# Out-projection in seven-product units, chained to the feed-forward of a hybrid decoder block

## The chip, the core and the metric

The kernel runs on one core of a Trainium2 chip. Its time is the device time in microseconds (us) of one execution, taken as the median of several runs. The engines have these names: PE is TensorE (matmul), PEld its weight load, DVE is VectorE, ACT is ScalarE, POOL is GpSimd, and SP is SyncE, which here only issues DMAs. [...]

## What is computed

One decoder layer over 2048 tokens with 1024 channels, all in float32:

```
h    = layer_norm(x, ln_in_g, ln_in_b)
proj = h @ w_in + b_in                      # split into q, k, v, su, sv
attn = sliding_window_attention(rope(q), rope(k), v, sinks)      # 512 wide
sgu  = spatial_gating(su, sv, ...)                               # 512 wide
mix  = concat([attn, sgu]) @ w_out + b_out                       # 1024 x 1024
h    = layer_norm(ALPHA * h + mix, ln_mix_g, ln_mix_b)
ffn  = (silu(h @ w_gate) * (h @ w_up)) @ w_down                  # 2816 wide
out  = layer_norm(ALPHA * h + ffn, ln_ffn_g, ln_ffn_b)
```

Each float32 operand of a matmul is split into a high part (rounded to the fp32r format, written by ACT) and a low part (the rest, written by DVE); a product is then three matmuls: high by high, high by low, low by high.

## The kernel before

The tokens are worked on in 16 tiles of 128 (`NT = 16`). The stages follow each other in time:

1. **Attention stage** (about 0 to 320 us). For each tile: load x, first layer norm (moments on DVE, scale and shift on ACT, affine part on POOL), eight transposes on PE (`x_transpose`), split, in-projection of q, k, v, attention. The split transposed h goes to DRAM (`hTd`), the attention's output too (`mixd[i][0]`).
2. **Gating stage** (`sgu_*`, to about 511 us). Eight groups of two tiles load `hTd` again and do the gating half; its output goes to `mixd[i][1]`. Beside it `load_wo` loads w_out and splits it.
3. **Out-projection** (line 791, `outproj`). One tile after another: `load_mix` brings the tile's mix back and splits it, 48 matmuls of 512 columns (8 blocks of 128 channels, 3 parts, 2 halves of the output) go into `pw` at line 798. Beside it `prep` loads x once more and computes ALPHA times the first layer norm, plus b_out, again (ACT line 139, DVE line 787, POOL line 788). Then line 800 adds `pw`, `normalize` takes the second layer norm (DVE lines 124 to 132, POOL's power at line 127), `affine` multiplies and adds on POOL (lines 142, 143), the result goes to `h2d`, and `h2_transpose` turns it with eight transposes into `h2T`, one tile later.
4. **Feed-forward.** A list of units, each one seven-product (Strassen-Winograd) multiply of 2 x 2 blocks. A gate/up unit `("g", h, f)` gives 128 channels of gate and of up for 1024 tokens; there are 44. A down unit `("d", g, j)` gives two token tiles over one group of hidden channels; there are 24. `unit` (line 924) runs the chain of line 823:

```python
CHAIN = (("a11", "X", True), ("s1", "Z", True), ("s2", "X", False), ("s4", "Z", False),
         ("s3", "X", False), ("a12", "Y", True), ("a22", "X", False))
```

Each product is 4 blocks by 3 parts, so 12 matmuls of 512 columns and 84 in a unit (63 where a group has three blocks). X, Z and Y are PSUM banks; "False" means that the product is accumulated onto what is in the bank, so the bank has to be read by the unit's hook before that product starts. After each product p of a unit, `after(p)` makes the left operand p of the next unit (`Left.make`: 7 splits and 4 sums or differences in a unit, each 128 x 512) and, where the right matrix changes, the right operand for p (`Right.make`: 28 splits and 12 differences in all, 128 x 512 each, into one `bc` buffer for each of seven operands).

The Tile framework simulates the schedule and writes a fixed order for each engine; a buffer is taken over as soon as the tiles that it overlaps are released. Between stages 3 and 4 the pools of the old stage are closed and those of the feed-forward (`psf`, eight PSUM banks; `bc`, `st`, `ot`) are opened. SP's DMA queue and POOL's DMA queue work in the order of issue.

Of the kernel before, what the change touches and what calls it, by code (L numbers as in the profile page):

```python
# [68 lines left out]
def hybrid_block(ctx, tc, x, pos, ln_in_g, ln_in_b, wqkv, wsu, wsv, b_qkv, b_su, b_sv, sinks,  # L69
                 sgu_g, sgu_b, wsT, bs, w_out, b_out, mix_g, mix_b, w_gate, w_up, w_down,  # L70
# [9 lines left out]
    hTd = [dram.tile([P, 2, KT, P], F32, name=f"hTd_{i}") for i in range(NT)]  # L80
    h2d = [dram.tile([P, D], F32, name=f"h2d_{i}") for i in range(NT)]
# [22 lines left out]
    sucol = base.tile([P, NH], F32, name="sucol")  # L104
    xrs = base.tile([P, NT], F32, name="xrs")
# [140 lines left out]
    SP.dma_start(bcol, sgu_b)  # L246

# [445 lines left out]
    wp = pool(front, "wp", 6)  # L693
# [17 lines left out]
    wo = {}  # L711

    def load_wo(k):
        r = raw(f"rwo{k}")
        SP.dma_start(r, w_out[k * P:(k + 1) * P, :])
        if k < 6:
            t = wp.tile([P, 2, D], F32R, tag="w", name=f"wo{k}")
            split_w(t[:, 0, :], t[:, 1, :], r, A, V)
            wo[k] = [t[:, :, :512], t[:, :, 512:]]
        else:  # L720
            wo[k] = []
            for c in range(2):
                t = ap_.tile([P, 2, 512], F32R, tag="a", name=f"wo{k}_{c}")
                split_w(t[:, 0, :], t[:, 1, :], r[:, c * 512:(c + 1) * 512], A, V)
                wo[k].append(t)

    mixs = {}

    def load_mix(i):
        r = raw(f"rm{i}")  # L730
        for j in range(2):
            SP.dma_start(r[:, j * 512:(j + 1) * 512], mixd[i][j].rearrange("p k t -> p (k t)"))
        m = [ap_.tile([P, 2, 512], F32R, tag="a", name=f"m{i}_{a}") for a in range(2)]
        for a in range(2):
            split_w(m[a][:, 0, :], m[a][:, 1, :], r[:, a * 512:(a + 1) * 512], A, V)
        mixs[i] = m

    for gi in range(NG):
# [10 lines left out]
        if gi + 1 == NG:  # L749
            load_wo(6)  # L750
            load_wo(7)
            load_mix(0)
# [9 lines left out]
        if 1 <= gi < 7:  # L762
            load_wo(gi - 1)
    a2.close()
    a2w.close()


    accp = pool(front, "accp", 4)
    trp = pool(front, "trp", 2)
    rp = pool(ctx, "rp", 4, side="right")  # L770
    wr = pool(ctx, "wr", 8, side="right")

    ag, ab = g_in, b_in
# [3 lines left out]
    V.scalar_tensor_tensor(ab, ab, ALPHA, rb, ALU.mult, ALU.add)
    mg = bcast(mix_g, "mg")
    mb = bcast(mix_b, "mb", ap_, "a")

    acc = {}

    def prep(i):
        ac = accp.tile([P, D], F32, tag="acc", name=f"acc{i}")
        SP.dma_start(ac, x[i * P:(i + 1) * P, :])
        x_normalize(ac, i)
        V.tensor_tensor(ac, ac, ag, ALU.mult)
        PL.tensor_tensor(ac, ac, ab, ALU.add)
        acc[i] = ac

    def outproj(i):
        m = mixs.pop(i)
# [78 lines left out]
    class Right:  # L871
# [52 lines left out]
    def unit(name, nk, left, right, hooks, after=None):  # L924
        bank = {}
        for n, (p, x_, first) in enumerate(CHAIN):
# [9 lines left out]
            if after:  # L936
                after(p)
# [229 lines left out]
```

## Time and profile before

| what | value |
|---|---|
| median of 3 runs | 2055.69 us (2055.38 to 2062.29) |
| profiled execution, its own time | 2054.37 us |
| span of the profiled execution | 2052.7 us |
| PE busy | 1956.4 us, 95% of the span |
| DVE busy | 1431.7 us, 70% |
| ACT busy | 754.0 us, 37% |
| POOL busy | 442.6 us, 22% |
| mean TensorE clock granted | 0.982 |

The span lies within the profiled execution's own time; 1.67 us are outside it. Matmuls are pipelined, so the mean of one (390 ns and more) is longer than the step from one to the next; the step is read from runs of many matmuls.

### The profile page before, as it was taken

How to read it: one execution, taken by the hardware profiler on the slowest of the kernel's cores; microseconds unless marked ns; L12 is line 12 of the kernel's file. 1: busy time of each engine (PE TensorE's matmuls, PEld its weight loads, DVE VectorE, ACT ScalarE, POOL GpSimd, SP SyncE). 2: the span in 40 equal slices, each digit the busy share in tenths (PEclk: the TensorE clock that was granted, in tenths of full speed). 3: DMA queues.
4: the chain of work that ended last, by engine and by line, in shares of the span. 5: the costliest groups of instructions: out<-in, count | busy, mean ns of one | idle time of the engine just before them, and what ended most of it. 6: DMA issues, size and time to landing. Idle time of an engine off the chain costs nothing.

```text
span 2052.7 us, 24699 instructions
## 1 busy us (share of the span) xinstructions
PE 1956.4 (95%) x9230; PEld 1611.6 (79%) x9230; DVE 1431.7 (70%) x2353; ACT 754.0 (37%) x1468; POOL 442.6 (22%) x378
## 2 busy tenths in 40 slices
PE   6898899999999779999999999999999999999997
PEld 4777778999778668888888888888888886887875
DVE  8888884745766875555555865555556869769997
ACT  4556663211322353333333533333334324224220
POOL 4576743110667510000000000000000000000212
PEclk9999999999999989999999999999999999999998
DMA  6224259855556342122122331221212656545432
GB/s 228 78 108 149 77 153 196 185 103 133 181 189 203 101 158 82 72 92 83 72 93 69 126 124 72 93 83 72 92 64 92 239 202 232 180 172 184 165 113 103
DMA packets 137008, 267.57 MB, mean 130 GB/s; under 512 B 8244, under 2 KB 79924, under 8 KB 133304
## 3 DMA queue, kind: packets, MB, share of 16 engines
q1 hardware_dynamic: 90024, 196.79, 28.2%
q0 software_dynamic: 46864, 69.21, 12.2%
q8 instruction: 72, 1.18, 0.3%
q14 instruction: 48, 0.39, 0.1%
HBM read 175.79 MB, written 90.18 MB: 130 GB/s over the span
## 4 chain that ended last, share of the span: by engine, by line
PE 65%; DVE 11%; issue 7%; DMA 4%; ACT 2%; POOL 2%; SPq 0%; POOLq 0%; DVEq 0%; ACTq 0%
PE X_g L932 21%; PE Z_g L932 11%; PE X_d L932 8%; PE Y_g L932 5%; PE Z_d L932 4%; PE pu L564 4%; PE pw L798 3%; PE psv L526 3%; PE Y_d L932 2%; DMA acc<-in_x 1%; DMA h2d<-acc 1%; ACT pb L404 1%; DVE da L1022 1%; DVE b_d L897 1%; PE pm L577 1%
## 5 line engine op out<-in xcount | busy, mean ns | idle before, releaser
L833 ACT ACTIVATE ws<-s 128x512 fp32r<-128x512 f32 x176 | 109.9, 627 | 314.6 <-PE Z_g L932 156.7
L982 POOL DMA_DIRECT2D aD<-x x44 | 23.6, 536 | 857.2 <-DVE x L980 837.8
L798 PE MATMUL pw<-wo,m 128*128 128x512 f32 x768 | 180.0, 394 | 0.0
L798 PEld LDWEIGHTS pw<-wo,m 128*128 128x128 f32 x768 | 144.1, 189 | 29.6
L834 DVE TENSOR_TENSOR ws<-s,ws 128x512 fp32r<-128x512 f32 x176 | 121.0, 690 | 54.1 <-ACT ws L833 52.9
L932 PE MATMUL Z_g<-t1t_h,ws 128*128 128x512 f32 x528 | 137.4, 396 | 0.3 <-DVE ws L834 0.3
L932 PE MATMUL Y_g<-b21t_h,wa 128*128 128x512 f32 x528 | 137.2, 394 | 0.0
L932 PE MATMUL X_g<-t2t_h,ws 128*128 128x512 f32 x528 | 130.8, 395 | 3.7 <-ACT x L962 3.7
L932 PE MATMUL Z_g<-b22t_h,ws 128*128 128x512 f32 x528 | 131.6, 398 | 1.7 <-ACT ws L833 1.7
L932 PE MATMUL X_g<-b11t_h,wa 128*128 128x512 f32 x528 | 131.7, 397 | 0.0
L932 PE MATMUL X_g<-t3t_h,ws 128*128 128x512 f32 x528 | 130.3, 395 | 0.2 <-ACT x L962 0.2
L932 PE MATMUL X_g<-t4t_h,wa 128*128 128x512 f32 x528 | 130.0, 395 | 0.0
L833 ACT ACTIVATE ws_d<-s_d 128x512 fp32r<-128x512 f32 (+1 forms) x96 | 55.7, 593 | 186.5 <-PE X_d L932 51.0
L932 PEld LDWEIGHTS Z_g<-b22t_h,ws 128*128 128x128 f32 x528 | 100.6, 191 | 25.8 <-ACT ws L833 2.2
L932 PEld LDWEIGHTS X_g<-t2t_h,ws 128*128 128x128 f32 x528 | 99.4, 188 | 27.2 <-ACT x L962 4.2
L834 DVE TENSOR_TENSOR wa<-rw,wa 128x512 fp32r<-128x512 f32 x132 | 90.2, 685 | 42.0 <-ACT wa L833 41.9
L932 PEld LDWEIGHTS Z_g<-t1t_h,ws 128*128 128x128 f32 x528 | 100.3, 190 | 24.5 <-DVE ws L834 1.0
L932 PEld LDWEIGHTS X_g<-b11t_h,wa 128*128 128x128 f32 x528 | 99.9, 189 | 23.2
L932 PEld LDWEIGHTS X_g<-t3t_h,ws 128*128 128x128 f32 x528 | 99.4, 188 | 23.8 <-ACT x L962 0.7
L932 PEld LDWEIGHTS Y_g<-b21t_h,wa 128*128 128x128 f32 x528 | 99.3, 188 | 23.5 <-ACT wa L833 0.2
L932 PEld LDWEIGHTS X_g<-t4t_h,wa 128*128 128x128 f32 x528 | 99.5, 188 | 23.1
L980 DVE TENSOR_TENSOR x<-X_g,x 128x512 f32<-128x512 f32 x44 | 30.4, 691 | 119.8 <-PE X_g L932 119.8
(224 smaller groups left out, 4111.0 us busy)
## 6 DMA issues: line engine op xcount, KB each, us to landing
rw<-in_w_gate SPq DMA_DIRECT2D x44, 512.0 KB, 3.8
rw<-in_w_up SPq DMA_DIRECT2D x44, 512.0 KB, 4.8
aD<-x POOLq DMA_DIRECT2D x44, 512.0 KB, 2.9
hTd<-hT SPq DMA_DIRECT2D x16, 1024.0 KB, 3.9
hTg<-hTd POOLq DMA_DIRECT2D x16, 1024.0 KB, 10.2
accd<-da POOLq DMA_DIRECT2D x32, 512.0 KB, 2.9
ra<-aD SPq DMA_DIRECT2D x16, 1024.0 KB, 7.2
da<-accd SPq DMA_DIRECT2D x32, 512.0 KB, 3.3
```

Of the source, the lines that this page charges most:

```text
L404: A.activation(pb, pb, AF.Exp, bias=nm[:, h:h + 1], scale=SCALE, accum_out=sm[:, h:h + 1])
L526: PE.matmul(pv_, t[:, a, k, :], wsv_t[k][:, b, :], start=(k == 0 and n == 0), stop=(k == KT - 1 and n == 2))
L564: PE.matmul(pu[:, j, :], wsu_t[k][:, a, hs], t[:, b, k, :], start=(k == 0 and n == 0), stop=(k == KT - 1 and n == 2))
L577: PE.matmul(pm[:, h].rearrange("p b t -> p (b t)"), z[:, a, hs], wsp[:, h].rearrange("p b t -> p (b t)"), start=(a == 0), stop=(a == 1))
L798: PE.matmul(po[:, c * 512:(c + 1) * 512], m[k // 4][:, a, kc], wo[k][c][:, b, :], start=(k == 0 and n == 0), stop=(k == KT - 1 and n == 2))
L833: A.activation(hi, src, AF.Copy)
L834: V.tensor_tensor(lo, src, f32b(hi), ALU.subtract)
L897: V.tensor_tensor(dst[:, k], a[:, k], b[:, k], ALU.subtract)
L932: PE.matmul(bank[x_], lt[:, a, k, :], rt[:, b, k, :], start=(first and k == 0 and m == 0), stop=(k == nk - 1 and m == 2), skip_group_check ...
L980: V.tensor_tensor(v["x1"], ps, v["x1"], ALU.mult)
L982: PL.dma_start(aD[g][h][:, e, :], v["o"].rearrange("p a t -> p (a t)"))
L1022: V.tensor_tensor(s, ps, s, ALU.add)
```

## The change

The out-projection becomes eight more units of the list, `("o", 0, j)`, ahead of the gate/up units: each is one seven-product multiply of two token tiles (left, from `mixd`) by w_out's four quarters (right). Three of the seven right operands (`b11`, `t1`, `t2`) are made in the gating stage by `wo_early`, in groups 2 and 4; the other four (`b22`, `t3`, `b21`, `t4`) are made when the gating stage has ended.

h, the output of the first layer norm, is stored to DRAM from the attention stage (`hd`, one DMA for each tile, in `x_transpose`), and loaded as the unit's accumulator with b_out/ALPHA added on POOL; `prep` goes. The second norm's scale and shift go to ACT (`o_hooks`, a new small DVE instruction makes the shift) and its result z, without the affine part, is stored as `zd`. `z_transpose` turns z in the next unit, after its products s4 and a12, and ACT applies the affine part by channel while it reads the transposes (`mcol`, 128 columns at a time). The affine part by rows, which the down units' accumulators need, is done later by `z_affine`: in gate/up units 3 to 18 of the first half, one tile in each unit is loaded, multiplied and added on POOL, and stored to `h2d` by POOL's queue.

The pools of the front stages move to the right side of SBUF, `wr` has 7 buffers instead of 8, and the last norm's rows are loaded later into the buffers of the second norm's. The diff, cut to its core:

```diff
+    hd = [dram.tile([P, D], F32, name=f"hd_{i}") for i in range(NT)]
+    zd = [dram.tile([P, D], F32, name=f"zd_{i}") for i in range(NT)]
...
-    bsvp = pool(front, "bsvp", 1)
+    pst = ExitStack()
+    ap_ = pool(front, "ap", 8, side="right")
+    rawp = pool(front, "rawp", 4, side="right")
+    cst = pool(front, "cst", 3, side="right")
+    bsvp = pool(front, "bsvp", 1, side="right")
     bsv = bsvp.tile([P, SGW], F32, name="bsv")
-    pst = ExitStack()
-    rawp = pool(front, "rawp", 4)
-    cst = pool(front, "cst", 3)
-    ap_ = pool(front, "ap", 8)
...
     def x_transpose(i):
         t = wk.tile([P, 2, KT, P], F32R, tag="hT", name=f"hT{i}")
+        SP.dma_start(hd[i], xt[i])
...
-    wp = pool(front, "wp", 6)
+    bc = {q: pool(ctx, "bc_" + q, 1) for q in ("b11", "t1", "t2")}
...
+    def wo_quarter(q, k0, n):
+        kk, c = {"b11": (0, 0), "b12": (0, 1), "b21": (1, 0), "b22": (1, 1)}[q]
+        r0 = (4 * kk + k0) * P
+        return w_out[r0:r0 + n * P, c * 512:(c + 1) * 512].rearrange("(k p) c -> p k c", p=P)
+
+    wo_t = {}
+
+    def wo_early(k0):
+        r = {}
+        for q in ("b11", "b12", "b22"):
+            r[q] = raw(f"rwo{q}{k0}").rearrange("p (k c) -> p k c", k=2)
+            SP.dma_start(r[q], wo_quarter(q, k0, 2))
+        for nm in ("b11", "t1", "t2"):
+            if nm != "b11":
+                V.tensor_tensor(r["b11"], r["b12" if nm == "t1" else "b22"], r["b11"],
+                                ALU.subtract)
+            if k0 == 0:
+                wo_t[nm] = bc[nm].tile([P, 2, 4, 512], F32R, tag="b", name=f"{nm}t_o")
+            t = wo_t[nm][:, :, k0:k0 + 2]
+            split_w(t[:, 0], t[:, 1], r["b11"], A, V)
...
-        if gi + 1 == NG:
-            load_wo(6)
-            load_wo(7)
-            load_mix(0)
...
-        if 1 <= gi < 7:
-            load_wo(gi - 1)
+        if gi in (2, 4):
+            wo_early(gi - 2)
...
+    pst.close()
+    front.close()
...
+    wr = pool(ctx, "wr", 7, side="right")
+    psf = pool(ctx, "psf", 8, space=PSUM)
+    st = pool(ctx, "st", 3)
+    ot = pool(ctx, "ot", 4)
+    bc.update({q: pool(ctx, "bc_" + q, 1) for q in ("b22", "t3", "b21", "t4")})
+    oo = ExitStack()
+    bop = pool(oo, "bop", 1)
+    trp = pool(oo, "trp", 2)
...
+            if q in self.t:
+                return
...
+                if "t2" not in r:
+                    r["t2"] = r["b11"]
+                    for k in range(self.nk):
+                        V.tensor_tensor(r["t2"][:, k], src[:, k], r["t2"][:, k], ALU.add)
...
+    bo = bop.tile([P, D], F32, name="bo")
+    SP.dma_start(bo, b_out.partition_broadcast(P))
+    A.activation(bo, bo, AF.Copy, scale=1.0 / ALPHA)
+
+    def load_m(j):
+        t = raw8(f"rm{j}").rearrange("p (e a c) -> p e a c", e=2, a=2)
+        for e in range(2):
+            for a in range(2):
+                SP.dma_start(t[:, e, a], mixd[2 * j + e][a].rearrange("p k t -> p (k t)"))
+        v = t.rearrange("p e a (k t) -> p e a k t", k=4)
+        return Left(f"o{j}", (v[:, 0, 0], v[:, 0, 1], v[:, 1, 0], v[:, 1, 1]), 4)
+
+    def o_right():
+        r = Right("o", lambda q, t: SP.dma_start(t, wo_quarter(q, 0, 4)), 4)
+        r.t.update(wo_t)
+        return r
+
+    hacc, zs = {}, {}
+
+    def load_h(j):
+        hacc[j] = []
+        for e in range(2):
+            t = ot.tile([P, D], F32, tag="o", name=f"hb{j}_{e}")
+            SP.dma_start(t, hd[2 * j + e])
+            PL.tensor_tensor(t, t, bo, ALU.add)
+            hacc[j].append(t)
+
+    def add_block(ac, seen, first, e, c, ps):
+        s = ac[e][:, c * 512:(c + 1) * 512]
+        if first and (e, c) not in seen:
+            V.scalar_tensor_tensor(s, s, ALPHA, ps, ALU.mult, ALU.add)
+        else:
+            V.tensor_tensor(s, ps, s, ALU.add)
+        seen.add((e, c))
+
+    def block_hooks(ac, first, done):
+        seen = set()
+
+        def add(e, c, ps):
+            add_block(ac, seen, first, e, c, ps)
+
+        def y(ps):
+            add(0, 0, ps)
+            done(0)
+
+        def x4(ps):
+            add(1, 0, ps)
+            done(1)
+
+        return {"a11": lambda ps: add(0, 0, ps), "s1": lambda ps: add(1, 1, ps),
+                "s2": lambda ps: add(0, 1, ps), "s4": lambda ps: add(0, 1, ps),
+                "s3": lambda ps: add(1, 1, ps), "a12": y, "a22": x4}
+
+    def o_hooks(j):
+        ac = hacc.pop(j)
+
+        def done(e):
+            i = 2 * j + e
+            mu, rs = moments(ac[e])
+            nmr = small.tile([P, 1], F32, tag="nmr", name=f"nmr{i}")
+            V.tensor_scalar(nmr, mu, rs, -1.0, ALU.mult, ALU.mult)
+            A.activation(ac[e], ac[e], AF.Identity, bias=nmr, scale=rs)
+            SP.dma_start(zd[i], ac[e])
+            zs[i] = ac[e]
+
+        return block_hooks(ac, True, done)
+
+    def z_transpose(i):
+        z = zs.pop(i)
+        for j in range(2):
+            ps = psf.tile([P, 512], F32, tag="f", name=f"ph{i}_{j}")
+            tr = trp.tile([P, 4, P], F32, tag="tr", name=f"tr{i}_{j}")
+            for k in range(4):
+                kk = 4 * j + k
+                PE.transpose(ps[:, k * P:(k + 1) * P], z[:, kk * P:(kk + 1) * P], ident)
+            for k in range(4):
+                kk = 4 * j + k
+                A.activation(tr[:, k], ps[:, k * P:(k + 1) * P], AF.Identity,
+                             bias=mcol[:, 1, kk:kk + 1], scale=mcol[:, 0, kk:kk + 1])
+            SP.dma_start(h2T[i // 4][:, 4 * j:4 * j + 4, (i % 4) * P:(i % 4 + 1) * P], tr)
+
+
+    def z_affine(i):
+        t = ot.tile([P, D], F32, tag="o", name=f"za{i}")
+        SP.dma_start(t, zd[i])
+        affine(t, t, fg[0], fg[1])
+        PL.dma_start(h2d[i], t)
...
+    units = [("o", 0, j) for j in range(NT // 2)]
+    units += [("g", h, f) for h in range(2) for f in range(NF)]
...
+    def load_out(u):
+        if u[0] == "o":
+            load_h(u[2])
+        elif u[0] == "d":
+            load_acc(*u[1:])
...
     ORDER = [p for p, _, _ in CHAIN]
-    prep(0)
-    lefts, rights = {}, {}
-    for i in range(NT):
-        if i + 1 < NT:
-            prep(i + 1)
-        outproj(i)
-        if i + 1 < NT:
-            load_mix(i + 1)
-        if i:
-            h2_transpose(i - 1)
-        if i == NT - 4:
-            lefts[0] = load_left(units[0])
-            rights[0] = load_right(units[0])
+    lefts, rights, fg = {}, {}, []
+
+    lefts[0] = load_left(units[0])
+    rights[0] = load_right(units[0])
+    load_out(units[0])
+    for n_, p in enumerate(ORDER):
+        lefts[0].make(p)
+        if n_ == 1:
             rights[0].fetch()
-    h2_transpose(NT - 1)
-    front.close()
-    pst.close()
-
-    psf = pool(ctx, "psf", 8, space=PSUM)
-    bc = {q: pool(ctx, "bc_" + q, 1) for q in BOF.values()}
-    st = pool(ctx, "st", 3)
-    ot = pool(ctx, "ot", 4)
-    fb_ = pool(ctx, "fb_", 1)
-
     for p in ORDER:
-        lefts[0].make(p)
         rights[0].make(p)
     lefts[1] = load_left(units[1])
-    fg = bcast(ffn_g, "fg", fb_, "fg")
-    fb = bcast(ffn_b, "fb", fb_, "fb")
     for n, u in enumerate(units):
-        new = n + 1 < len(units) and units[n + 1][:2] != u[:2]
+        last = n + 1 == len(units)
+        new = not last and units[n + 1][:2] != u[:2]
         if new:
             rights[n + 1] = load_right(units[n + 1])
             rights[n + 1].fetch()
-        elif n + 1 < len(units):
+        elif not last:
             rights[n + 1] = rights[n]
 
         def after(p):
-            if n + 1 < len(units):
+            if not last:
                 lefts[n + 1].make(p)
             if new:
                 rights[n + 1].make(p)
-
-        if u[0] == "g":
-            hooks, nk = gu_hooks(*u[1:]), 4
-        else:
-            if n and units[n - 1][0] == "g":
-                load_acc(*u[1:])
-            if n + 1 < len(units):
-                load_acc(*units[n + 1][1:])
-            hooks, nk = d_hooks(*u[1:]), GROUPS[u[1]][1] // 2
+            if 0 < n <= NT // 2 and p in ("s4", "a12"):
+                z_transpose(2 * (n - 1) + (p == "a12"))
+
+        if u == ("g", 0, 1):
+            oo.close()
+            fb_ = pool(ctx, "fb_", 2)
+            fg = [bcast(mix_g, "mg", fb_, "f"), bcast(mix_b, "mb", fb_, "f")]
+        if u == ("d", 1, 0):
+            fg = [bcast(ffn_g, "fg", fb_, "f"), bcast(ffn_b, "fb", fb_, "f")]
+        if u[0] == "g" and u[1] == 0 and 3 <= u[2] < 3 + NT:
+            z_affine(u[2] - 3)
+        if not last:
+            load_out(units[n + 1])
+        hooks = {"o": lambda _, j: o_hooks(j), "g": gu_hooks, "d": d_hooks}[u[0]](*u[1:])
+        nk = GROUPS[u[1]][1] // 2 if u[0] == "d" else 4
         unit("_".join(str(x_) for x_ in u), nk, lefts.pop(n), rights.pop(n), hooks, after)
```

## Rows read from the trace of the kernel before

**Rows 1.** The page: busy time of each engine; granted clock over 40 slices.

```profile
span 2052.7 us, 24699 instructions
...
PE 1956.4 (95%) x9230; PEld 1611.6 (79%) x9230; DVE 1431.7 (70%) x2353; ACT 754.0 (37%) x1468; POOL 442.6 (22%) x378
...
PEclk9999999999999989999999999999999999999998
```

**Rows 2.** Windows by stage: length, busy time (instructions) by engine, clock, DMA share, GB/s.

```profile
346.00:500.00 154.00, 153.68 (x1006) 140.52 (x1004) 95.15 (x237) 28.38 (x50) 22.62 (x23) 1.00 0.75 151
...
511.20:759.70 248.50, 220.87 (x996) 180.18 (x995) 187.13 (x224) 82.74 (x127) 135.80 (x64) 0.95 0.50 169
...
780.00:1140.00 360.00, 360.00 (x1551) 291.92 (x1550) 195.31 (x295) 127.35 (x221) 10.13 (x19) 1.00 0.22 81
...
1900.00:2020.00 120.00, 119.59 (x515) 96.56 (x515) 114.41 (x188) 27.32 (x46) 26.44 (x23) 1.00 0.39 135
```

**Rows 3.** Windows with line 798 (out-projection) alone: PE, PEld, then clock, DMA.

```profile
511.20:759.70 248.50, 178.66 (x764) 143.16 (x762) 0.95 0.50 169
700.00:759.70 59.70, 6.04 (x27) 4.68 (x25) 0.80 0.41 138
```

**Rows 4.** The same with line 932 (units) alone.

```profile
700.00:759.70 59.70, 28.49 (x104) 21.73 (x105) 0.80 0.41 138
```

**Rows 5.** The chain that ended last, pieces in order of time: start, length, what.

```profile
639.15 10.92 PE pw L798 x48
...
761.25 2.79 PE X_g L932 x12
```

**Rows 6.** Timeline, end of gating, one tile's transposes, turn to feed-forward: start, length, engine.

```profile
510.16 0.99 PE L577 MATMUL pm<-wsp,z 128*128 128x256 f32 x7
...
513.38 0.69 DVE L588 TENSOR_TENSOR sg<-sg,u 128x512 f32<-128x512 f32 x1
...
638.11 1.04 PE L811 MATMUL ph<-ident,acc 128*128 128x128 f32 x8
...
638.91 1.40 PE L798 MATMUL pw<-wo,m 128*128 128x512 f32 x5
...
711.16 1.97 PE L811 MATMUL ph<-ident,acc 128*128 128x128 f32 x8 [5.12 <-POOL acc L143]
...
723.80 1.97 PE L811 MATMUL ph<-ident,acc 128*128 128x128 f32 x8 [10.67 <-POOL acc L143]
...
725.42 3.71 PE L932 MATMUL X_g<-b11t_h,wa 128*128 128x512 f32 x12
```

**Rows 7.** Groups by line: count, busy us, mean ns, idle before.

```profile
L834 DVE TENSOR_TENSOR ws<-s,ws 128x512 fp32r<-128x512 f32 x176 | 121.0, 690 | 54.1 <-ACT ws L833 52.9
...
L143 POOL TENSOR_TENSOR acc<-acc,mb 128x1024 f32<-128x1024 f32 x16 | 43.2, 2702 | 1.2
L142 POOL TENSOR_TENSOR acc<-acc,mg 128x1024 f32<-128x1024 f32 x16 | 42.4, 2647 | 14.9 <-DVE acc L132 14.9
...
L132 DVE TENSOR_SCALAR acc<-acc,mv,rs 128x1024 f32<-128x1024 f32 x16 | 15.0, 940 | 12.9 <-POOL rs L127 12.9
...
L125 DVE BATCH_NORM_AGGREGATE mv<-st 128x2 f32<-128x12 f32 (+1 forms) x64 | 12.5, 196 | 1.2
```

**Rows 8.** Single lines: shortest, median, longest in ns.

```profile
L166 DVE TENSOR_TENSOR m<-rm,m x32: 679/1448/2892, 495.8 to 689.5; 128x512 fp32r<-128x512 f32 x32
...
L124 DVE BATCH_NORM_STATS2 st<-acc x32: 668/678/689, 533.2 to 716.3; 128x6 f32<-128x512 f32 x32
```

**Rows 9.** Windows at turns of the right matrix and at the gating stage's end.

```profile
1140.00:1200.00 60.00, 59.78 (x258) 48.17 (x257) 55.45 (x92) 35.00 (x64) 1.60 (x3) 1.00 0.42 147
1700.00:1760.00 60.00, 55.44 (x224) 42.43 (x223) 57.04 (x95) 25.38 (x47) 3.19 (x6) 0.97 0.68 225
...
497.00:515.00 18.00, 18.00 (x133) 17.14 (x132) 11.31 (x31) 3.42 (x7) 1.01 (x2) 1.00 0.60 197
```

**Rows 10.** DMA issues: size and median us from issue to landing.

```profile
aD<-x POOLq DMA_DIRECT2D x44, 512.0 KB, 2.9
...
acc<-in_x SPq DMA_DIRECT2D x16, 512.0 KB, 4.1
```

More of the change, by code (lines that the diff above doesn't have):

```diff
@@ L69, in hybrid_block @@
 def hybrid_block(ctx, tc, x, pos, ln_in_g, ln_in_b, wqkv, wsu, wsv, b_qkv, b_su, b_sv, sinks,
-                 sgu_g, sgu_b, wsT, bs, w_out, b_out, mix_g, mix_b, w_gate, w_up, w_down,
+                 sgu_g, sgu_b, wsT, bs, w_out, b_out, mix_col, mix_g, mix_b, w_gate, w_up, w_down,
                  ffn_g, ffn_b, out):
@@ L104, in hybrid_block @@
     sucol = base.tile([P, NH], F32, name="sucol")
+    mcol = base.tile([P, 2, KT], F32, name="mcol")
     xrs = base.tile([P, NT], F32, name="xrs")
@@ L777, in hybrid_block @@
[L777 to L792, printed above, removed]
-        po = ps2.tile([P, D], F32, tag="two", name=f"pw{i}")
-        for k in range(KT):
-            kc = slice((k % 4) * P, (k % 4 + 1) * P)
-            for n, (a, b) in enumerate(((0, 0), (0, 1), (1, 0))):
-                for c in range(2):
-                    PE.matmul(po[:, c * 512:(c + 1) * 512], m[k // 4][:, a, kc], wo[k][c][:, b, :],
-                              start=(k == 0 and n == 0), stop=(k == KT - 1 and n == 2))
-        V.tensor_tensor(acc[i], po, acc[i], ALU.add)
-        normalize(acc[i], acc[i])
-        affine(acc[i], acc[i], mg, mb)
-        SP.dma_start(h2d[i], acc[i])
@@ L805, in h2_transpose @@
-    def h2_transpose(i):
-        ac = acc.pop(i)
-        tr = trp.tile([P, KT, P], F32, tag="tr", name=f"tr{i}")
-        for j in range(2):
-            ps = ps1.tile([P, 512], F32, tag="one", name=f"ph{i}_{j}")
-            for k in range(4):
-                PE.transpose(ps[:, k * P:(k + 1) * P], ac[:, (4 * j + k) * P:(4 * j + k + 1) * P],
-                             ident)
-            A.activation(tr[:, 4 * j:4 * j + 4, :], ps.rearrange("p (k t) -> p k t", k=4), AF.Copy)
-        SP.dma_start(h2T[i // 4][:, :, (i % 4) * P:(i % 4 + 1) * P], tr)
+    wr = pool(ctx, "wr", 7, side="right")
@@ L1014, in d_hooks @@
         ac = dacc.pop((g, j))
-        seen = set()
-        def add(e, c, ps):
-            s = ac[e][:, c * 512:(c + 1) * 512]
-            if g == 0 and (e, c) not in seen:
-                V.scalar_tensor_tensor(s, s, ALPHA, ps, ALU.mult, ALU.add)
-            else:
-                V.tensor_tensor(s, ps, s, ALU.add)
-            seen.add((e, c))
         def done(e):
@@ L1030, in done @@
                 last = i == NT - 1
-                ln_fused(ac[e], ac[e], fg, fb, 2 if last else 1,
+                ln_fused(ac[e], ac[e], fg[0], fg[1], 2 if last else 1,
                          lambda cs: PL.dma_start(out[i * P:(i + 1) * P, cs], ac[e][:, cs]))
-        def y(ps):
-            add(0, 0, ps)
-            done(0)
-        def x4(ps):
-            add(1, 0, ps)
-            done(1)
-        return {"a11": lambda ps: add(0, 0, ps), "s1": lambda ps: add(1, 1, ps),
-                "s2": lambda ps: add(0, 1, ps), "s4": lambda ps: add(0, 1, ps),
-                "s3": lambda ps: add(1, 1, ps), "a12": y, "a22": x4}
@@ L1046, in hybrid_block @@
-    units = [("g", h, f) for h in range(2) for f in range(NF)]
+        return block_hooks(ac, g == 0, done)
+    units = [("o", 0, j) for j in range(NT // 2)]
+    units += [("g", h, f) for h in range(2) for f in range(NF)]
     units += [("d", g, j) for g in range(len(GROUPS)) for j in range(NT // 2)]
     def load_left(u):
-        return load_w(*u[1:]) if u[0] == "g" else load_a(*u[1:])
+        return {"o": lambda _, j: load_m(j), "g": load_w, "d": load_a}[u[0]](*u[1:])
     def load_right(u):
-        return h_right(u[1]) if u[0] == "g" else d_right(u[1])
```

33 lines of the change are left out of this document (3 added, 30 removed).

## The prediction

> **What bounds the kernel now.** The page comes first: PE is busy 95% of the span at a clock of 0.98, DVE 70%, and the clock row dips in few slices [rows 1]. So PE sets the time almost everywhere; a change pays only if PE gets less work or loses less time between stages. The windows by stage say where that is: gating keeps PE busy 153.68 of 154 us, gate/up units 360 of 360, and even the last down units, with DVE at 114.41 of 120, keep PE at 119.59 [rows 2]. Read that last row with care: a chain of units hides a DVE that is 95% busy. The stretch from the end of gating to the first units is the exception: 248.5 us with a clock of 0.95 [rows 2].
>
> What that stretch should cost comes from the chain: 48 out-projection matmuls take 10.92 us, so 0.2275 each, and 12 of a unit 2.79, so 0.2325 [rows 5]. A tile's eight transposes take 638.91 - 638.11 = 0.8 us of PE [rows 6]. Between 511.2 and 759.7 lie 764 out-projection matmuls (173.8 us), 16 tiles' transposes (12.8) and 104 unit matmuls (24.2), together 210.8 us [rows 3, 4]. The other **37.7 us** are lost. Of these 59.7 - 27 x 0.2275 - 2 x 0.8 - 24.2 = 27.8 fall behind 700 us, in the turn to the feed-forward: PE waits 5.1 and 10.7 us for POOL's affine part before the last two tiles' transposes, the first unit starts at 725.42, and the clock is 0.80 [rows 3, 4, 6]. The other 10 are spread over the sixteen tiles.
>
> **The change, part by part.**
>
> PE's products: 768 x 0.2275 = 174.7 us become 8 x 84 x 0.2325 = 156.2. That gives **18.5 us**. The transposes stay 16 x 0.8 in number and cost.
>
> The old losses go with the old loop: **37.7 us**. New ones take their place; each follows.
>
> Out-projection units: PE needs 84 x 0.2325 + 2 x 0.8 = 21.1 us for one with two tiles' transposes. DVE does 11 left-operand instructions and 7 adds of 128 x 512 at 0.69, four statistics at 0.68, and for each tile an aggregate of 0.20 and two of about 0.2 more: 12.4 + 2.7 + 1.2 = 16.3 us [rows 7, 8]. That is 77%, less than the 95% under which PE lost 0.41 of 120 us [rows 2]. ACT has 7 splits, two scalings and sixteen reads of 128 columns; I don't need its sum, since ACT is far from full [rows 2]. Two things can stretch DVE. A DVE subtraction of two SBUF operands took 0.68 us at best, 1.45 in the median and 2.89 at worst beside POOL's long adds, while statistics, with one operand, stayed between 0.67 and 0.69 [rows 8]. POOL's b_out adds are two of about 2.7 us in a unit [rows 7], so DVE can lose up to 5.4 us a unit. And the shift waits for POOL's power, as line 132 did, 12.9 us over 16 tiles, so 1.6 us a unit [rows 7]. At the full price DVE has 16.3 + 5.4 + 1.6 = 23.3 us, 2.2 over PE's 21.1, or 18 us over eight units; at the least, nothing, because PE's products have several banks ahead. I take **2 us**, nearer to nothing: only half of those subtractions were much lengthened while POOL worked 135.80 of 248.5 us [rows 2, 8], and here it works about 6 of 21.
>
> [...]
>
> Start of the chain: nothing precedes it that could cover it. Gating's last matmul ends at 511.15, its last DVE instruction at 514.1 [rows 6]. Then DVE still has to make four right operands (16 splits, 12 differences and sums: 28 x 0.69 = 19.3 us) and the first left operands (7.6), with six adds between (4.1): 31.0 us. In 497 to 515 it was busy only 11.31 of 18 [rows 9], so some 6.7 of this can be done before; 24.3 remain, to 538.4, and a last product of 2.8 ends the unit at 541.2. PE alone would end it at 511.2 + 19.5 = 530.7. So 10.5 us are lost, and I add 2.5 for loads that wait for one of four raw buffers (4.1 us from issue to landing [rows 10]): **13 us**. From below: in the old turn PE did 20 products of the next unit by the time the first one ended (104 against 84 [rows 4]); the same here gives back 4.7, so about 6. From above: the old turn's 27.8.
>
> Turn from out-projection to gate/up: the right operands of h are made while the last unit runs, 28 splits and 12 differences, 40 x 0.69 = 27.6 us of DVE. Their source was stored four units earlier, so no wait on the last tiles is left. Over the last unit and two gate/up units PE needs 21.1 + 2 x 19.5 + 1.6 = 61.7 us, DVE 16.3 + 2 x 10.6 + 27.6 = 65.1 (10.6 is 195.31/360 of a unit [rows 2]). The turn inside gate/up lost PE 0.22 us of 60, the one inside down 4.56 and a little clock [rows 9]. This one is nearer the second: **5 us**, bounds 0.2 and 7.
>
> Late affine parts: 16 gate/up units get a load, two POOL instructions of 2.70 and 2.65, and a store that moves from SP's to POOL's queue [rows 7]. DVE is 54% and POOL 3% busy there [rows 2], which is the cover. Queued behind on POOL is the unit's own store of its result, which frees an `ot` buffer; it lands in 2.9 us [rows 10], so about 4 us after the unit's end. The next unit's second bank is ready 5.6 us after that end and must be read by 8.4. One POOL instruction in the way fits, two are late by some 1.6 us. **3 us** over all sixteen, from 0 to the rival's price.
>
> At nothing: the store of h in the attention stage (16 more DMAs of 512 KB on SP's queue; the raw buffer that each holds about 4 us longer is due again only after an iteration of some 17 us); the early split of three operands (10 DVE instructions of about 1.2 us for 10 before, under a DVE that is 95.15 of 154 us busy [rows 2]); seven `wr` buffers (each needed 16.7 us after it is free). If that cover is gone, each costs what it takes, 3 us or less. The removed reload of x, its norm and its three long elementwise passes cost the end nothing beyond the 10 us already counted.
>
> Sum: 18.5 + 37.7 - 2 - 13 - 5 - 3 = 33.2 us less. Against the profiled execution's own 2054.37 that is 2021.2. The median of the runs lies 1.3 above that execution, so I forecast **2022 us**, with 2012 to 2032 for this case alone.
>
> **Rivals.**
>
> B, start and turn are hidden: the chain reaches ahead as at its other turns; start 6, turn 0.2, nothing else. Gain 50, so 2006 us. For it speaks the turn inside gate/up, against it DVE's 31 us at the start.
>
> C, out-projection units bound by DVE: the full 18 us in place of 2, so 2038, and with a start some way to its upper bound 2044. For it the 1.45 us median of the two-operand subtractions; against it that POOL works far less here.
>
> D, the boundary only moves: start and turn each cost what the old turn did, 2 x 27.8, and no gain is left: 2055. For it that the old turn shows what preparing operands for a fresh chain costs; against it that three of seven are made before, and that the turn no longer waits for POOL.
>
> E, slower: the late affine parts stop gate/up. [...] It ends slower than the median by 0.5% from (33.2 + 3 + 10.3)/16 = 2.9 us a unit. For it the 2.89 us subtractions; against it DVE's free 46% and that a stalled DVE has eight banks before PE stops.
>
> **How the numbers follow.** My case has 0.50, B 0.17, C 0.15, D 0.08, E 0.10. About 0.5% (10.3 us, 2045.4 to 2066) is what a measurement of this kernel can tell from no change. A, B and C are faster: 0.82; D is the same: 0.08; E slower: 0.10. The range leaves out D and E and reaches from just under B to the upper end of C: 2003 to 2045.
>
> **What would show it.** In the profile after: 672 matmuls of a step of 0.2325 in eight units of about 21 us; the first unit ending near 541, 30 us after gating, with DVE full; gate/up starting some 165 to 185 us after gating ends, without a pause of 5 us before it and with the clock at or near 1; gate/up units of 19.5 us also where POOL works on the late affine parts; every later turn as before. Units of 23 us or more with a full DVE would mean C; gate/up units 3 to 18 longer than the others, with PE waiting for reads of its banks, E; a first unit ending behind 550, D. I would be wrong most easily in the start, which no row of before shows, and in how the framework's fixed order places POOL's long instructions.

## The result, and the profile after

The changed kernel takes 2045.24 us in the median of four runs (2042.68 to 2046.87) beside 2056.49 for the kernel before on the same chip: a ratio of 0.9939, with a 95% interval of 0.9917 to 0.996. It is faster by about 11 us, where 33 were forecast, and lies just above the range, which ended at 2045.

The page of the changed kernel, its busy times and the granted clock in 40 slices ([rows 1] before):

```profile
PE 1944.6 (95%) x9134; PEld 1588.1 (78%) x9134; DVE 1487.1 (73%) x2460; ACT 798.7 (39%) x1600; POOL 458.1 (22%) x394
PEclk9899999999799999999999999999999999999999
```

PEclk is the share of TensorE's clock that was granted, here in tenths and in windows as a mean. Behind the first slices it dips once, to 7 at the eleventh, where the out-projection starts. The windows around it, by stage ([rows 2] and [rows 9] before):

```profile
core 0: us, PE busy (x) PEld busy (x) DVE busy (x) ACT busy (x) POOL busy (x), PEclk, DMA share, GB/s
500.00:520.00 20.00, 16.86 (x115) 15.45 (x114) 12.45 (x32) 5.72 (x11) 0.55 (x1) 0.87 0.71 250
520.00:540.00 20.00, 10.55 (x30) 6.59 (x28) 17.04 (x20) 8.25 (x15) 13.57 (x4) 0.67 0.61 223
540.00:560.00 20.00, 16.87 (x61) 13.27 (x61) 18.82 (x32) 4.31 (x8) 0.00 (x0) 0.77 0.46 158
560.00:580.00 20.00, 19.97 (x95) 16.02 (x94) 16.43 (x35) 13.96 (x29) 5.05 (x4) 1.00 0.55 176
580.00:680.00 100.00, 100.00 (x469) 81.53 (x468) 73.61 (x131) 56.53 (x114) 27.75 (x19) 1.00 0.63 198
...
700.00:720.00 20.00, 17.73 (x78) 13.23 (x76) 20.00 (x35) 15.50 (x32) 0.00 (x0) 1.00 0.44 153
720.00:740.00 20.00, 14.51 (x61) 11.24 (x61) 18.32 (x37) 12.99 (x23) 2.01 (x2) 0.83 0.62 213
...
780.00:1140.00 360.00, 360.00 (x1545) 289.14 (x1544) 241.61 (x301) 127.38 (x228) 98.72 (x64) 1.00 0.35 130
```

Three things are to be seen. From 580 to 680 us the out-projection units run at PE's own speed, with DVE at 74%. From 780 to 1140 PE doesn't lose a microsecond, though POOL now works 98.72 us there on the late affine parts. What is lost lies in two places: 500 to 560, with 30 matmuls in one window of 20 us, and 700 to 740, with DVE full.

The products alone (line 897, PE and PEld) give the size:

```profile
512.40:580.00 67.60, 50.40 (x177) 37.44 (x178) 0.80 0.51 176
580.00:690.00 110.00, 103.71 (x436) 80.69 (x435) 1.00 0.63 198
690.00:745.00 55.00, 44.49 (x175) 33.14 (x174) 0.94 0.57 192
820.00:1100.00 280.00, 280.00 (x1201) 224.89 (x1200) 1.00 0.37 137
```

In the first row 177 products at 0.2333 and 16 transposes at 0.1 are 42.9 us; 24.7 of the 67.6 are lost. Below, "loss" is the same thing taken matmul by matmul: what lies between the starts of two matmuls beyond the first one's own step, where that is over 0.06 us, summed over a stretch. So measured, the start (500 to 580 us) lost 25.2 us and the turn to gate/up (680 to 780) 11.5; before, the three stretches of this stage lost 3.4, 6.5 and 28.4, which is the 37.7 of the prediction within 0.6. A product that was lengthened while less of the clock was granted counts with what it took longer: in the start PEclk was 0.50 from 514.91 to 531.97 us and from 538.81 to 549.00, and 27 products took 0.43 us there in place of 0.2333, which is 5.2 of the 25.2 us.

The timeline of the start: PE, ACT, DVE, POOL and SP's issues (the number in brackets is the idle time before, and who ended it):

```profile
511.27 1.10 PE L582 MATMUL pm<-wsp,z 128*128 128x256 f32 x8
...
512.20 0.63 ACT L792 ACTIVATE wa_o<-rm 128x512 fp32r<-128x512 f32 x1
...
514.31 1.28 DVE L856 TENSOR_TENSOR b_o<-b_o 128x512 f32<-128x512 f32 x2
...
515.51 0.68 DVE L793 TENSOR_TENSOR wa_o<-rm,wa_o 128x512 fp32r<-128x512 f32 x1
...
516.25 4.63 PE L897 MATMUL X_o<-b11t_o,wa_o 128*128 128x512 f32 x10 [2.63 <-DVE wa_o L793]
...
521.10 1.89 DVE L851 TENSOR_TENSOR t3t_o<-b_o,t3t_o 128x512 fp32r<-128x512 f32 x3
...
522.02 1.80 SPq L928 DMA_DIRECT2D hb<-hd  x4
522.91 0.68 DVE L816 TENSOR_TENSOR s_o<-rm 128x512 f32<-128x512 f32 x1
...
525.60 13.57 POOL L929 TENSOR_TENSOR hb<-hb,bo 128x1024 f32<-128x1024 f32 x4 [23.39 <-DMA hb<-hd]
...
531.27 0.69 DVE L935 SCALAR_TENSOR_TENSOR hb<-hb,X_o 128x512 f32<-128x512 f32 x1 [2.26 <-POOL hb L929]
531.87 2.27 DVE L825 TENSOR_TENSOR s_o<-rm,s_o 128x512 f32<-128x512 f32 x1
532.48 2.96 PE L897 MATMUL X_o<-t2t_o,ws_o 128*128 128x512 f32 x12
...
534.85 4.87 DVE L793 TENSOR_TENSOR ws_o<-s_o,ws_o 128x512 fp32r<-128x512 f32 x2 [0.70 <-ACT ws_o L792]
...
559.34 2.96 PE L897 MATMUL X_o<-t4t_o,wa_o 128*128 128x512 f32 x12
```

The first left operand is split at 512.20, while gating's last products run, and DVE's first instruction of the chain starts at 514.31: nothing of the chain's DVE work was done before. From then to 560 DVE is idle for only 4.1 us, so its work sets the pace of the start. DVE makes t3, which the fifth product needs, ahead of s1, which the second needs. And POOL's adds of b_out stand on the path: the first addition waits 2.26 us for them, and three DVE instructions with two SBUF inputs take 7.14 us (2.27 and 4.87) in place of about 2. The last line is the last product of the first unit; it ends at 562.

At the turn, who waited for whom between 690 and 760 us (sum, times, longest):

```profile
PE X_g L897 <- ACT x L1027: 4.8, 1, 4.8
ACT b21t_h L850 <- DMA b_h<-h2T: 4.3, 1, 4.3
PE X_g L897 <- DVE t2t_h L851: 1.6, 1, 1.6
```

ACT's wait for the load of b21 did not hold up DVE, which was busy in all of the 20 us from 700 to 720 and had no pause up to 734.

### The profile page after: what moved, and what is told of

The parts are those of the page before. It is cut to its first block, busy times and chain, and to the rows that moved or that the text cites. A ratio compares the mean times of both kernels' runs of the same rounds, so it can differ in the third digit from the quotient of the medians.

```text
span 2043.7 us, 24808 instructions
## 1 busy us (share of the span) xinstructions
PE 1944.6 (95%) x9134; PEld 1588.1 (78%) x9134; DVE 1487.1 (73%) x2460; ACT 798.7 (39%) x1600; POOL 458.1 (22%) x394
## 4 chain that ended last, share of the span: by engine, by line
PE 53%; issue 24%; DVE 10%; ACT 2%; POOL 1%; DMA 1%; POOLq 0%; SPq 0%; DVEq 0%; ACTq 0%
PE X_g L897 11%; PE X_d L897 10%; PE Z_g L897 5%; PE Z_d L897 5%; PE pu L569 4%; PE psv L531 4%; PE X_o L897 4%; PE Y_g L897 3%; PE Y_d L897 2%; PE Z_o L897 2%; ACT pb L409 1%; PE Y_o L897 1%; DVE b_d L856 1%; PE pm L582 1%; POOL aD L1036 1%
## 5 line engine op out<-in xcount | busy, mean ns | idle before, releaser
L793 DVE TENSOR_TENSOR ws<-s,ws 128x512 fp32r<-128x512 f32 x176 | 136.1, 776 | 74.7 <-ACT ws L792 73.8
L792 ACT ACTIVATE wa<-rw 128x512 fp32r<-128x512 f32 x132 | 82.5, 628 | 216.1 <-PE X_g L897 186.5
L897 PEld LDWEIGHTS Z_g<-b22t_h,ws 128*128 128x128 f32 x528 | 98.9, 187 | 24.7 <-DVE ws L793 0.5
L897 PEld LDWEIGHTS Y_g<-b21t_h,wa 128*128 128x128 f32 x528 | 98.9, 187 | 24.2
L130 POOL TENSOR_TENSOR rs<-ve,nhalf 128x1 f32<-128x1 f32 x48 | 51.4, 1071 | 267.1 <-DVE ve L129 261.3
```

What stands on the lines that cost most here:

```text
L130: PL.tensor_tensor(rs, ve, nhalf, ALU.pow)
L792: A.activation(hi, src, AF.Copy)
L793: V.tensor_tensor(lo, src, f32b(hi), ALU.subtract)
L897: PE.matmul(bank[x_], lt[:, a, k, :], rt[:, b, k, :], start=(first and k == 0 and m == 0), stop=(k == nk - 1 and m == 2), skip_group_check ...
```

## Experiments

Ratios are to the kernel before, run beside each; "start" and "turn" are the losses defined above, in us.

| run | median us | ratio (95%) | start | turn |
|---|---|---|---|---|
| the change | 2045.2 | 0.9939 (0.9917 to 0.996) | 25.2 | 11.5 |
| s_reuse | 2033.8 | 0.988 (0.986 to 0.990) | 12.7 | 14.0 |
| s_hqueue | 2048.6 | 0.9959 (0.9945 to 0.9973) | 27.4 | 13.0 |
| s_hq_nobias | 2036.5 | 0.9897 (0.9883 to 0.9912) | 17.9 | 11.3 |
| s_all | 2027.0 | 0.9855 (0.9838 to 0.9871) | 7.1 | 11.3 |
| o_order | 2043.3 | 0.9936 (0.9919 to 0.9953) | 24.2 | 12.0 |
| v_q | 2042.6 | 0.9935 (0.9918 to 0.9953) | 18.7 | 12.8 |
| v_qd | 2040.4 | 0.9922 (0.9905 to 0.9938) | 8.3 | 13.6 |
| t_rp5 | 2067.5 | 1.0053 (1.0038 to 1.0068) | 28.7 | 15.3 |
| t_reuse | 2048.5 | 0.9953 (0.9938 to 0.9968) | 24.9 | 2.4 |
| a_align | 2009.6 | 0.9768 (0.9752 to 0.9784) | 24.7 | 11.4 |
| b_align | 2030.7 | 0.9866 (0.9851 to 0.988) | | |
| v_best | 2000.0 | 0.9719 (0.9703 to 0.9736) | 13.4 | 13.4 |
| a_pad224 | 2010.5 | 0.9781 (0.9752 to 0.9809) | | |
| a_pad416 | 2043.9 | 0.9944 (0.9921 to 0.9966) | | |

### The start: work, h, or order

Theory one was the prediction's: DVE's work on late right operands. Its rivals: h comes late, and the fixed order.

s_reuse, tiles made before in place of four late ones:

```
+        r.t.update(b22=wo_t["b11"], t3=wo_t["t1"], b21=wo_t["t2"], t4=wo_t["b11"])
+        r.fetch = lambda: None
+        r.get = lambda q: None
```

> Leaves out: the right operands b22, t3, b21 and t4 of the out-projection are not made; tiles made before take their places, so 16 ACT splits and 28 DVE instructions (19.3 us of DVE) and three loads vanish from the start, and the out-projection multiplies by wrong matrices. Everything else of the units is as in the changed kernel, in which the start lost PE 25.2 us between 500 and 580 us and the median is 2045.2 us. Theory one, DVE's work on late right operands sets the start: the loss falls by 15 to 19 us, to 6 to 10, the first unit ends near 545, and the time is 2026 to 2030 us. Theory two, the first addition waits for h (its load stands behind gating's last stores on SP's queue and POOL's adds of b_out follow) : the first addition still comes at about 531, the loss stays at 16 or more, and the time is 2036 to 2043 us.

s_hqueue has the first of these two edits, s_hq_nobias both:

```
-            SP.dma_start(t, hd[2 * j + e])
+            (PL if j == 0 else SP).dma_start(t, hd[2 * j + e])
-            PL.tensor_tensor(t, t, bo, ALU.add)
+            if j > 1:
+                PL.tensor_tensor(t, t, bo, ALU.add)
```

> The two loads of h for the first unit go out on POOL's queue, which is free at the end of gating, in place of SP's, where they stood behind the two stores of gating's last results until 522.02. Nothing is left out. Theory one (DVE's work on right operands): the loss of 25.2 us at the start moves by 3 us at most, so 2042 to 2048 us. Theory two (h comes late): POOL's adds begin some 8 us earlier, the first addition comes near 522 in place of 531, and the loss falls by 5 to 9 us, to 2036 to 2040 us.

> As the run with the loads of h on POOL's queue, and POOL's adds of b_out are left out for the first two units (four tiles lack b_out), so that no long POOL instruction stands ahead of the first additions or beside DVE's subtractions of two SBUF operands. Theory one: DVE's instructions get their 0.68 us back (some 8 us of lengthening between 531 and 545), the work on right operands stays: the loss falls by 4 to 8 us, 2037 to 2041 us. Theory two: the first addition comes as soon as the first product ends and h has landed (near 518), the loss falls by 12 us or more, 2030 to 2034 us.

s_all joins the three edits.

> Both together: loads of h on POOL's queue, no adds of b_out in the first two units, and no right operands made at the start (it leaves out what these two leave out). Both theories: what is left is the first left operands of two units (some 15 us of DVE over 40 us) and the first additions, so a loss of 3 to 8 us in place of 25.2, and 2023 to 2028 us. Over 10 us of loss left would mean a third cause, such as the order in which gating's last instructions and the first left operands stand on DVE and ACT.

Without the 28 DVE instructions (and the 16 ACT splits and three loads that go with them) the loss falls by 12.5 us, less than the 15 to 19 of theory one and more than theory two allows; without the adds by 7.3, or by 9.5 beside s_hqueue, from which only the adds set it apart; without both by 18.1. The move to POOL's queue failed as an experiment: h came no earlier (POOL's first add began at 529.2 there, 525.6 in the changed kernel), so it tells nothing of an earlier h. That h was not the limit is seen in s_hq_nobias: no add stood before it, and the first addition still came 19.1 us after gating's last product, against 18.9. What changed there is DVE's speed; its instructions in the stretch of the long ones above:

```profile
527.76 1.28 DVE L793 TENSOR_TENSOR ws_o<-s_o,ws_o 128x512 fp32r<-128x512 f32 x2
528.96 0.68 DVE L936 SCALAR_TENSOR_TENSOR hb<-hb,X_o 128x512 f32<-128x512 f32 x1
529.56 0.68 DVE L825 TENSOR_TENSOR s_o<-rm,s_o 128x512 f32<-128x512 f32 x1
```

Then the order. o_order gives the first sums a place that is free early, and queues each late right operand behind the left one that is needed before it (the core of the edit):

```
+            if name == "o_0_0" and 0 < n < 5:
+                a, v = ins[n + 1]
+                with tc.issue_after(a), tc.issue_after(v):
+                    right.make(CHAIN[n + 2][0])
```

> Nothing is left out; only the order at the start changes. The first unit's left operands get a place in SBUF that is free before gating ends, and ACT and DVE make each late right operand only behind the left operand that is needed before it (in the changed kernel t3 and b22 stood ahead of s1, which the second product waits for). Theory one, the amount of DVE work between gating and the end of the first unit sets the start: the same work in another order, so a loss of 21 to 26 us in place of 25.2 and 2041 to 2046 us. Theory three, the fixed order sets it: products two and three run at once and hide part of the work, the loss falls by 8 us or more, to 17 or less, and the time to 2037 us or less.

v_q also adds b_out to h of the first four tiles during gating, and v_qd takes t3's and t4's differences there (the cores of the edits):

```
+        for e in range(2):
+            t = raw(f"he{j}_{e}")
+            SP.dma_start(t, hd[2 * j + e])
+            PL.tensor_tensor(t, t, b, ALU.add)
+            PL.dma_start(hd[2 * j + e], t)
...
+        for nm, dst, a, b in (("t3", "b12", "b22", "b12"), ("t4", "b21", "b11", "b21")):
+            V.tensor_tensor(r[dst], r[a], r[b], ALU.subtract)
+            PL.dma_start(wod[nm][:, k0:k0 + 2, :], r[dst])
```

In v_qd the difference for t4 has the opposite sign, which leaves every instruction as long as it is; v_best has it right.

> The order of the run before, and b_out is added to h of the first four tiles in gating's last groups, on POOL, where PE has work, so that the first two units need no long POOL instruction; nothing is left out. The run without these adds had a loss of 17.9 us at the start and 2036.5 us. Theory one (amount of DVE work): order brings little on top, a loss of 14 to 18 us, 2033 to 2037 us. Theory three (order): 10 us or less, 2029 us or less. If gating pays for the adds, its stretch from 346 to 500 us loses PE over 1 us.

> As the run before, and the differences that make t3 and t4 are taken in gating, where DVE was 62% busy, and stored; the start loads them ready, so that 12 DVE instructions (8.3 us) fewer stand there. Nothing is left out. Theory one: the loss falls by 6 to 8 us against the run before, to 8 to 12 us, and the time by as much. Theory three: by 3 us or less, since with the right order the work was hidden.

Another order of the same work leaves 24.2 of 25.2 us, and without the adds it changes as little (18.7 in v_q, 17.9 in s_hq_nobias): this order is no remedy, and the old one not the cause. 8.3 us of DVE less leave 10.4 us less; 5.8 of these are 31 products that were lengthened in v_q, where PEclk was 0.86, 0.89 and 0.91 in the windows of 20 us from 520 to 580; in v_qd it was 1.00 there, and none was. So theory one holds, with POOL's adds as a second part. Both gains were paid back in gating, which lost 7.0 us in v_q and 12.3 in v_qd (0.7 in the changed kernel), so the times of both runs missed what was expected. In v_qd ACT waited 7.53 us for b_out with the next Gelu behind it; in v_q the adds met gating's norms:

```profile
379.77 4.84 POOL L744 TENSOR_TENSOR he<-he,bo 128x1024 f32<-128x1024 f32 x2
...
379.83 2.58 DVE L135 TENSOR_SCALAR gv<-gv,mv,rs 128x512 f32<-128x512 f32 x1 [0.47 <-POOL rs L130]
382.45 2.44 DVE L168 CAST z<-gv 128x512 fp32r<-128x512 f32 x1
```

Without an add beside them these two take 0.55 and 0.43 us. The copy reads one tile only, so not just instructions with two SBUF inputs were lengthened here.

### The turn

t_rp5 is `rp` 4 to 5 and `wr` 7 to 5 buffers.

> Five raw buffers in place of four and five buffers for left operands in place of seven (the same space); nothing is left out. It is for the turn to gate/up, which lost PE 11.5 us between 680 and 780 us in the changed kernel. Theory A, the last quarter of h (b21) comes late for want of a raw buffer (issued 712.87, ACT waited 4.29 us for it): it is issued 15 us earlier, the loss of the turn falls to 3 to 6 us, the time to 2036 to 2040 us. Theory B, DVE has more to do around the turn than PE: the loss stays at 10 to 13 us and the time at 2044 to 2047 us.

t_reuse, for the first half of the tokens:

```
...
+                if BOF[p] in ("b11", "t1", "t2"):
+                    make(p)
+                else:
+                    r.t[BOF[p]] = r.t["b11"]
...
```

> Leaves out: for the first half of the tokens the right operands b22, t3, b21 and t4 of h are not made (b11's tile takes their places, so gate and up are wrong there), which takes 16 ACT splits, 28 DVE instructions and the late load of b21 out of the turn from out-projection to gate/up. The turn lost PE 11.5 us between 680 and 780 us, and an earlier load of b21 alone did not lower that. Theory B, DVE has more to do around the turn than PE: the loss falls to 4 us or less, 2035 to 2039 us. Rival: the last tiles' norms, the transposes that wait for them and ACT's order hold the turn: 8 us or more remain, 2041 to 2046 us.

With five raw buffers ACT no longer waits for b21, and the turn still loses 15.3. By itself that does not clear the load, since this run has two buffers fewer for left operands: it is slower by 22 us, with 4.5 us lost at the turn inside gate/up, where the changed kernel loses none, and some 9 more in the down units. (That it is for want of these buffers is likely and was not tried alone.) DVE's unbroken work in the changed kernel's turn does. Without the work, and without the load, the turn loses 2.4 us; its windows, and the turn inside gate/up:

```profile
700.00:720.00 20.00, 19.31 (x86) 15.02 (x85) 17.89 (x33) 12.53 (x24) 0.55 (x1) 1.00 0.67 230
720.00:740.00 20.00, 19.22 (x92) 15.74 (x92) 10.84 (x18) 13.51 (x29) 1.48 (x2) 1.00 0.69 233
...
1140.00:1160.00 20.00, 15.00 (x42) 9.12 (x41) 18.94 (x32) 12.90 (x23) 0.53 (x1) 0.74 0.23 79
```

DVE falls from 20.00 and 18.32 us to 17.89 and 10.84: its work on the right operands is the cause. The gain was lost again at 1140, where this edit keeps b11's only tile in use up to the last product of a half (12.3 us); so the total says nothing, and the stretch does.

### The step of the products

Units of gate and up took 19.6 us in place of 19.5, with or without affine parts: products took 0.2333, not 0.2325. In both kernels the step goes with where tiles begin in SBUF. The traces hold no addresses, the programs do: modulo 512 bytes the units' weights begin at 480 in both, the moving tiles (the right operands) at 352 before and at 0 after, because `mcol` and the small buffers of the new shift, 160 bytes, stand ahead of them. a_align:

```
+    pool(ctx, "pad", 1).tile([P, 120], F32, name="pad")
     bc = {q: pool(ctx, "bc_" + q, 1) for q in ("b11", "t1", "t2")}
```

b_align does the same in the kernel before with 32 columns, a_pad224 and a_pad416 in the changed one with 56 and 104.

> The changed kernel with 480 bytes of SBUF left free below the right operands, and nothing else. In both kernels' traces a 128x512 product takes 0.2275 us where the tile of its weights and its moving tile begin at the same place modulo 512 bytes (before: out-projection, both at 352; after: gating's odd groups, both at 480, and the attention's projections) and 0.2325 to 0.234 where they don't (units before: 480 and 352, 0.2325; units after: 480 and 0, 0.2333). With the 480 bytes the units' tiles all begin at 480. Theory P, the place sets the step: 0.2275 in all 6216 unit products, 0.0058 each, so 30 to 36 us less than the changed kernel, 2009 to 2016 us, and gate/up units of 19.1 us in place of 19.6. Rival: the step differs for another reason (the order of instructions, the beat of their loading), and 2043 to 2047 us remain.

> The kernel before with 128 bytes of SBUF left free below the right operands, so that they begin at 480 modulo 512 as the weights' tiles do, in place of 352. Nothing else is changed. Theory P: 5544 unit products at 0.2275 in place of 0.2325, 22 to 28 us less than the kernel before, 2028 to 2034 us. Rival: no change, 2054 to 2058 us.

> The changed kernel with 224 bytes left free, so that right operands begin at 224 and the weights' tiles at 480 modulo 512: the same place modulo 256. If 256 bytes are the period that counts, the step is 0.2267 as with 480 bytes and the time 2006 to 2013 us; if the period is 512 (or more), 0.2325 to 0.234 and 2039 to 2047 us.

> The changed kernel with 416 bytes left free: right operands begin at 416, the weights' tiles at 480 modulo 512, the same place modulo 64 only. If a period of 64 bytes is what counts, 0.2267 and 2006 to 2013 us; if it is a longer one, 0.2325 to 0.234 and 2039 to 2047 us.

Twelve products of one group in the timeline of the changed kernel, and of a_align:

```profile
917.57 2.96 PE L897 MATMUL X_g<-t4t_h,wa 128*128 128x512 f32 x12
```

```profile
908.38 2.88 PE L898 MATMUL X_g<-t4t_h,wa 128*128 128x512 f32 x12
```

With the last product's 0.395 and 0.389 us taken off, eleven steps are 2.565 and 2.49 us: 0.2332 and 0.2265. The other rows read 2.88 in b_align and a_pad224 and 2.96 in a_pad416. So in these runs two tiles that began at the same place modulo 256 bytes gave the short step, 0.2265; 32, 64 or 128 bytes apart gave 0.2325 to 0.2334. The pads change nothing else: each engine's instructions stand in the same order in the traces with and without them, so the order is not the cause. The kernel before shows the same within one stage: gating's groups load their weights in turn into a tile at 352 and one at 480, while the moving tile stays at 352:

```profile
412.37 11.08 PE L526 MATMUL psv<-wsv,hTg 128*128 128x512 f32 x48
...
436.65 11.32 PE L526 MATMUL psv<-wsv,hTg 128*128 128x512 f32 x48
```

With 0.39 us taken off for the last product, 47 steps are 0.2274 us each in the first and 0.2326 in the second.

### What the runs point to

v_best joins the place, the order, v_qd's moved work, and a fixed place for the adds:

```
+            with tc.issue_after(mark["pow"]):
+                PL.tensor_tensor(t, t, b, ALU.add)
```

> What the runs so far point to, with nothing left out: tiles at the same place modulo 512; the start's left operands ahead of its late right ones; b_out added to h of the first four tiles behind gating's groups five and six (the run that did it without a fixed place lost 6.3 us where ACT and DVE waited for it); the differences for t3 and t4 taken in gating. Theories one and P together: units at 0.2275, a loss of 8 to 11 us at the start in place of 25.2, gating's loss under 3 us: 1990 to 1999 us. If gating pays for the moved work as before (11 us), 2000 to 2006 us; if the place of the tiles does nothing, 2026 us or more.

It takes 2000.0 us, 2.8% less than before, and leaves nothing out. Its windows in gating, where the adds now stand, and at the start:

```profile
460.00:480.00 20.00, 20.00 (x126) 18.11 (x126) 13.04 (x26) 3.10 (x6) 8.72 (x7) 1.00 0.99 179
480.00:500.00 20.00, 20.00 (x136) 18.55 (x135) 10.41 (x29) 3.90 (x7) 6.98 (x6) 1.00 0.28 105
...
520.00:540.00 20.00, 19.02 (x74) 14.04 (x73) 18.37 (x31) 10.34 (x21) 0.00 (x0) 0.93 0.79 261
```

PE stays full beside POOL's 8.72 and 6.98 us; gating loses 2.6 us in all. The start lost 13.4, against 8.3 in v_qd (3.0 of it are products that were lengthened, with PEclk at 0.93 from 520 to 540 and 0.91 from 560 to 580, of which v_qd, at 1.00, had none; the rest is open), and 2000.0 is just above the 1990 to 1999 expected.

## Why the prediction was wrong

The mechanism that the prediction named, DVE's work on operands, was right; its size was not. **The step that failed is the start of the chain**, 13 us forecast and 25.2 measured, with the first unit ending at 562 and not 541; past 550, which the prediction had named as the sign of its rival D. The start alone did come near D's price (27.8); the turn did not. Three parts of that term were wrong. "Some 6.7 of this can be done before": nothing was. POOL's adds of b_out were priced in the units, where they cost next to nothing, and not at the start, where four of them met DVE's work: 5.2 us of lengthening (7.14 in place of 1.96) and a wait of 2.26. And nothing stood in it for the clock, though the 27 products of 0.43 us, with PEclk at 0.50, make 5.2 of the 25.2 us.

Two things went the other way. Back to back, DVE starts such an instruction every 0.60 us (four took 2.48), so the 45 that were priced at 0.69 cost 4 us less; and by the end of the first unit PE had done 24 products of the second, 5.6 us, which the prediction had put into its lower bound alone. So 13 + 6.7 + 5.2 is 24.9, but that it comes so near is in part luck: the terms left out cancel, and no run takes them apart. The runs bear out the adds (7.3 us without them), and v_qd that DVE work taken ahead of gating's end lessens the loss. That the free time of DVE between 497 and 515 could have been used is not shown: in o_order the place of the first sums was free, and the first of them still came at 512.71, behind gating's last DVE instruction.

For the adds the prediction had the rows: two-input subtractions lengthened beside POOL's long adds, statistics not [rows 8]. The changed kernel shows the lengthening too: 2.27 us beside POOL's adds, and 0.68 for the same instruction without them in s_hq_nobias. It was priced in the units and not at the start. Of the instructions that read one tile the statistics stayed at 0.69 us or less [rows 8], while the copy in v_q took 2.44 in place of 0.43.

**The turn**, 5 forecast, cost 11.5, above its bound of 7. The prediction had DVE's sum (65.1 us against PE's 61.7) and still took a value near the turn inside down [rows 9]; that DVE is the cause is shown by t_reuse and by its 20.00 busy us of 20.

**The products.** 672 at 0.2333 are 156.8 us (156.2 forecast), so 17.9 of the 18.5. But 0.0008 more in each of the 5544 products of gate/up and down is 4.4 us that no term held: the tiles moved.

**Better than forecast:** the out-projection units lost 0.7 us in place of 2, the late affine parts nothing in place of 3. No run shows the rival's price that bounded this term from above, a wait for the whole of both POOL instructions in each unit: PE was busy for 360.00 of 360 us beside POOL's 98.72. Rivals C and E are refuted by the windows 580 to 680 and 780 to 1140; B by the start. Seven `wr` buffers cost gate/up nothing; five, with a fifth raw buffer, went with 22 us more. Gating's last product came 1.2 us later: attention took 3.8 longer, where the store of h was put at nothing, and gating 2.6 less. Whether the store did it was not tried.

Together: 33.2 - 12.2 (start) - 6.5 (turn) - 5.0 (step, all 6216) + 1.3 (units) + 3 (affine) - 1.2 (up to gating's end) - 1.9 (more loss in the down units) = 10.7. The two profiled executions differ by 2054.37 - 2045.42 = 9.0, the medians by 11.3; 1.3 of what is left lies behind the last product, from which the end came 15.0 us later and not 13.7.

With the tiles of both kernels in the same place the change is worth 2030.7 - 2009.6 = 21.1 us. There the products save 96 x 0.2267 = 21.8 in place of 18.5, and 33.2 + 3.3 - 12.2 - 6.5 + 1.3 + 3 - 1.2 - 1.9 = 19.0. Of the 22 us that were missing, most lay in the start and the turn, and part of the rest in where the tiles fell.

## What to carry to other kernels

Price the start of a chain as all of the work its operands need, at the speed that this work has beside everything else that starts there (here 7.14 us in place of 1.96 beside POOL's adds), and count as done before only what the program places ahead of the last stage's tail (a free place in SBUF alone did not bring it there). Before judging a change of a PE-bound kernel, compare the step of its products: a change that moves tiles can move every product, as here from 0.2325 to 0.2333 us. A loss removed at one turn is read in that turn's windows, since an edit may hand it to the next.

## What was not expected of the hardware

In these runs the time of an fp32r product of 128x512 went with where its weights and its moving tile begin relative to each other. In the units, whose weights begin at 480 modulo 512: equal modulo 256 bytes (0 or 256 apart modulo 512) 0.2267 us, 32 or 64 apart 0.2333, 128 apart 0.2325. In gating the weights' tile moved and the moving one stayed, with the same effect (0.2274 and 0.2326). It is 2.5 to 3%, and 36 us of this kernel (2045.2 to 2009.6). Why is open: no run shows what makes the place matter.
